# Last expert gathered an expert earlier, expert 30's part added in the last accumulation, biases in four parts, two more ring places

## The chip, the cores and the metric

The kernel runs on one core of a Trainium2 chip. The metric is the device time of one execution in microseconds (us). Three executions of the kernel before took 1175.88, 1176.34 and 1177.59 us. The profiled execution, from which all rows below come, took 1176.17 us, of which its trace covers a span of 1174.3 us from the first to the last instruction. All arithmetic is float32 unless a line says otherwise.

## The reference

256 tokens of 1024 numbers pass one layer: an attention-like mixer (an SSD group and an MLA group beside each other), then a mixture of experts. The second half is what the change touches.

```python
logits = h @ w_router + b_router
top_vals, top_idx = lax.top_k(logits, 4)          # 4 of 32 experts for each token
gates = softmax(top_vals)
...                                               # for each expert, its tokens xb and gates g:
gu = xb @ w_gate_up[e] + b_gate_up[e]             # 1024 -> 2 x 1024
glu = minimum(gu[:, :1024], 7.0); lin = clip(gu[:, 1024:], -7.0, 7.0)
act = glu * sigmoid(1.702 * glu) * (lin + 1.0)
y = act @ w_down[e] + b_down[e]                   # 1024 -> 1024
f += y * g                                        # added to the token's row
...
x = x + g2 * rms_norm(f, post_ffn_norm)
```

The weights of one expert are 8 MiB (w_gate_up) and 4 MiB (w_down). All 32 experts are read, so 384 MiB of the 427 MiB that the kernel reads are theirs.

## The kernel before, in words

**Front.** The mixer runs first, some 195 us. Its weights come as tiles of 1 MiB, and so do those of the experts. SP issues every load, in the order of one list, into one queue. A tile of the list has a place in SBUF. `Stream` (lines 72 to 105) holds the free places: a load is written into the program as soon as a place is free in program order. The mixer has 7 places (w0 to w6). While it ends, it hands on eleven buffers of its own (lines 1082, 1138, 1150), so the experts have 18. The order in which instructions stand on SP, DVE and ACT is then set by a scheduler that simulates the program; SP's loads go where the simulation has their place free. On PE the order is that of the program text from line 544 on.

**An expert, e.** Its tokens (up to 64; the rare rest is handled in a branch, `overflow`) are gathered by a matmul with a one-hot matrix, `gather(e)` (8 instructions at line 1173, each float32 matmul being two), transposed and scaled in `gathered(e)` (line 1181). `up` (line 1194) multiplies by the eight tiles gu0 to gu7 of w_gate_up; for each tile 4 matmuls, 8 instructions. `act` (lines 1207 to 1233) transposes the result on PE (line 1214, "tp"), and DVE and ACT make the activation `ac`. `down` (line 1242, "py") multiplies by the four tiles dn0 to dn6 of w_down. Rows of 64 slots are used: one matmul fills 64 of the 128 PSUM partitions.

**The loop.** Lines 1417 to 1469 run over the experts. In iteration e PE does: up on gu0 and gu1 of e, gather(e+1), down(e-1), up on gu2 and gu3, the transposes for e+1, up on gu4 to gu7, the branch, the transposes of act(e). After every even expert the results of the two experts before are added to the tokens: `scatter` (lines 1271 to 1278, "pc") makes four matmuls of 128 x 512, each followed by an addition to `acc` on DVE. The matrix for it, `gt`, comes from `spread_cols` (DVE) and `spread_mats` (four transposes, line 1266, and a copy on ACT). Expert 30 is different: down(29) is done at the start of its iteration, before up. In iteration 31 PE does down(30), copies it to `yl`, and scatters it alone (line 1437).

**The biases of w_down** (b_down) are added once for all experts: a matmul of the gates (32 experts as rows) with b_down, in the scatter of expert 24, ahead of each of its four matmuls (line 1276, 32 rows of the array). b_down and the gain of the last norm are loaded together as the tile `end`, ahead of expert 22's weights; it keeps its place in the ring to the end of the program.

**The end.** w_down of expert 31 comes in pieces by columns: 0 to 511, 512 to 767, 768 to 1023 (`parts`, line 1474). For each of the three and each half t of the tokens there is a PSUM bank `fin`. A matmul with the identity first puts `acc` into it (lines 1450 and 1498), and the last scatter (line 1483) adds expert 31. ACT sums the squares from `fin` (line 1484), DVE multiplies `fin` by the gain (line 1478), then come the norm, the addition to x and four stores.

Of the kernel before, what the change touches and what calls it, by code (L numbers as in the profile page):

```python
# [9 lines left out]
F32 = mybir.dt.float32  # L10
# [5 lines left out]
OP = mybir.AluOpType  # L16
# [5 lines left out]
P = 128  # L22
TT = S // P
# [83 lines left out]
def body(ctx, tc, a, out, ne=NE):  # L107
    nc = tc.nc
# [4 lines left out]
    def tl(shape, name, tag=None, dt=F32):  # L113
        tag = tag or name
        return sb.tile(shape, dt, tag=tag, name=name)
# [167 lines left out]
        return f  # L283

    for e in range(ne):
        if e == ne - 10:
            st_.want("end", ld_end)
        for k in range(KT):
            st_.want(f"gu{e}_{k}", ld(lambda t: t, w_gu[e][:, k, :]))
        for k in range(0, FT, 2):  # L290
            if e < ne - 1:
                st_.want(f"dn{e}_{k}", ld(halves, w_dn[e][:, k // 2]))
            else:
                st_.want(f"dn{e}_{k}", ld_last(k))
# [865 lines left out]

    mp = ctx.enter_context(tc.tile_pool(name="mp", bufs=1, space=PSUM))
    acc = tl([P, TT, D], "acc", "f1")
    iota = cst[:, CIO : CIO + CAP]

    def gather(e):
# [95 lines left out]
    def spread_mats(go):  # L1261
# [5 lines left out]
        gt = tl([P, 2, TT, P], "gtm", "bgr")  # L1267
        A.copy(gt, pg)
        return gt

    def scatter(lhs, rhs, bias=None, tag="pc", chs=(0, 1), ts=range(TT)):
        for t in ts:
            for ch in chs:
                pc = mp.tile([P, 512], F32, tag=tag, name="pc", bufs=2)
                if bias is not None:
                    T.matmul(pc, bias[:, t, :], end[0:NE, D + ch * 512 : D + ch * 512 + 512], start=True, stop=False)
                T.matmul(pc, lhs(t, ch), rhs(ch), start=bias is None, stop=True)  # L1277
                V.tensor_tensor(acc[:, t, ch * 512 : ch * 512 + 512], acc[:, t, ch * 512 : ch * 512 + 512], pc, op=OP.add)  # L1278

    def warm(n):  # L1280
# [136 lines left out]
    for e in range(ne):  # L1417
        wg = [st_.take(f"gu{e}_{k}") for k in range(KT)]
        wdp, wd = wd, weights_down(e)
        ahead = e in (0, 2, 3, last)  # L1420
        if e == last - 1:
            finish_down(e - 1, ac, wdp)
        if e == last:
            py = down(e - 1, ac, wdp, 0)
            yl = tl([P, 512], "yl", "pv2")
            A.copy(yl, py)
        gu = halves_of_up()
        tc.mark_branch_hint_location(f"more{e}", engines=[mybir.EngineType.PE])
        up(gu, xT, wg, range(0, 2))
        if ahead:  # L1430
            overflow(e, wg, wd, f"pr{(e + ahead) % 2}")
            for k in range(0, 2):
                st_.done(f"gu{e}_{k}")
        if e < last:
            xg = gather(e + 1)
        if e == last:
            scatter(lambda t, ch: gt[64 * ch : 64 * ch + 64, 0, t, :], lambda ch: yl[64 * ch : 64 * ch + 64, :])
        elif 0 < e < last - 1:
            finish_down(e - 1, ac, wdp)
        up(gu, xT, wg, range(2, 4))  # L1440
        if e < last:
            xTn = gathered(e + 1, xg)
        if e % 2 == 0:
            go = spread_cols((e, e, e + 1, e + 1) if e == last - 1 else (e, e + 1, e + 1, e))
        if e == ne - 7:
            g2b = gain()
        if e == last:
            fin = {(t, 1): mp.tile([P, 512], F32, tag="pc", name="fin", bufs=2) for t in range(TT)}
            for t in range(TT):
                T.matmul(fin[t, 1][:, 0:256], ident, acc[:, t, 512:768], start=True, stop=False)  # L1450
        up(gu, xT, wg, range(4, 8))
        xT = xTn
# [5 lines left out]
        if e == ne - 8:  # L1458
            end = st_.take("end")
            bias = gates_by_expert()  # L1460
        pair = e > 0 and e % 2 == 0
        if pair and e < last - 1:
            scatter(lambda t, ch: gt[:, ch, t, :], lambda ch: comb[ch], bias)
            bias = None
# [3 lines left out]
        if e % 2 == 0:  # L1468
            gt = spread_mats(go)


    tc.keep_in_program_order(A.activation(epsw, epsc, AF.Sqrt))
# [2 lines left out]

    def gained(t, i):
        c0, w = parts[i]
        V.tensor_tensor(acc[:, t, c0 : c0 + w], fin[t, i][:, 0:w], g2b[:, c0 : c0 + w], op=OP.mult)  # L1478

    def last_scatter(t, i, now=True):  # L1480
        c0, w = parts[i]
        fv = fin[t, i][:, 0:w]
        T.matmul(fv, gt[:, 1, t, :], yl[i], start=False, stop=True)  # L1483
        A.activation(scr[:, 0:w], fv, AF.Square, accum_out=ssf[:, t, i : i + 1])  # L1484
        if i == 0:
            V.tensor_scalar(ssf[:, t, 0:1], ssf[:, t, 0:1], 1.0 / D, EPS, op0=OP.mult, op1=OP.add)
        elif i == 1:
            V.scalar_tensor_tensor(ssf[:, t, 1:2], ssf[:, t, 1:2], 1.0 / D, ssf[:, t, 0:1], op0=OP.mult, op1=OP.add)  # L1488
        else:
            A.activation(ssf[:, t, 2:3], ssf[:, t, 2:3], AF.Sqrt, bias=ssf[:, t, 1:2], scale=1.0 / D)  # L1490
        if now:
            gained(t, i)

    for t in range(TT):
        for i, tag in ((0, "gu"), (2, "tp")):
            c0, w = parts[i]
            fin[t, i] = mp.tile([P, 512], F32, tag=tag, name="fin", bufs=2)
            T.matmul(fin[t, i][:, 0:w], ident, acc[:, t, c0 : c0 + w], start=True, stop=False)  # L1498
    ordered.__exit__(None, None, None)
    ordered = tc.manual_schedule(engines={mybir.EngineType.PE, mybir.EngineType.Activation, mybir.EngineType.DVE})  # L1500
    ordered.__enter__()
    yl = []
    for i, (c0, w) in enumerate(parts):
        py = mp.tile([P, 512], F32, tag=("py", "sm", "py")[i], name="pyl")
        for f0 in (0, 4):
            for f in range(f0, f0 + 4):
                g = f % 2
                wv = wd(f, c0 // 512)[:, c0 % 512 : c0 % 512 + w]
                T.matmul(py[64 * g : 64 * g + 64, 0:w], ac[:, f, :], wv, start=f < 2, stop=f >= 6)  # L1509
        yl.append(tl([P, w], f"yl{i}", ("pv2", "bn", "md1")[i]))  # L1510
        A.copy(yl[i], py[:, 0:w])
        if i:
            for t in range(TT):
                last_scatter(t, i - 1)
# [42 lines left out]
```

## Time and profile before

| | |
|---|---|
| median of three executions | 1176.34 us |
| the profiled execution | 1176.17 us, span 1174.3 us |
| PE busy (matmuls) | 1074.3 us, 91% of the span |
| DVE, ACT, POOL busy | 448.6, 190.8, 66.4 us |
| moved by DMA | 449.23 MB, 383 GB/s over the span |
| mean granted clock of TensorE | 0.961 of full speed |

PE (the matmul engine) and the DMA queue are both busy nearly throughout, so a share says little on which of them a stretch waits for. What is to be read is, for each stretch, whether the queue's rate falls (then it waits for a free place, and PE sets the pace), or whether PE stands still for a tile (then the queue sets it). [...]

### The profile page before, as it was taken

How to read it: one execution, taken by the hardware profiler on the slowest of the kernel's cores; microseconds unless marked ns; L12 is line 12 of the kernel's file. 1: busy time of each engine (PE TensorE's matmuls, PEld its weight loads, DVE VectorE, ACT ScalarE, POOL GpSimd, SP SyncE). 2: the span in 40 equal slices, each digit the busy share in tenths (PEclk: the TensorE clock that was granted, in tenths of full speed). 3: DMA queues.
4: the chain of work that ended last, by engine and by line, in shares of the span. 5: the costliest groups of instructions: out<-in, count | busy, mean ns of one | idle time of the engine just before them, and what ended most of it. 6: DMA issues, size and time to landing. Idle time of an engine off the chain costs nothing. (4 is left out here: it accounts for less than half of the span.)

```text
span 1174.3 us, 13394 instructions
## 1 busy us (share of the span) xinstructions
PE 1074.3 (91%) x5079; PEld 456.9 (39%) x5082; DVE 448.6 (38%) x921; ACT 190.8 (16%) x364; POOL 66.4 (6%) x68
## 2 busy tenths in 40 slices
PE   5899998989999999898989898989798999999897
PEld 4886774333333333232333232323233233333333
DVE  6968844333232323232323232323223133323233
ACT  5265442111110001010101010101001000111003
POOL 1254440000000000000000000000000000000000
PEclk9899999999999999898999898989899979999898
DMA  9968799779989999999999999999999998999992
GB/s 325 326 257 338 253 377 366 307 291 403 414 360 419 420 420 419 420 420 420 420 420 421 419 421 420 419 421 420 407 420 420 420 388 337 420 420 419 421 409 83
DMA packets 79915, 449.23 MB, mean 383 GB/s; under 512 B 10385, under 2 KB 23166, under 8 KB 29090
## 3 DMA queue, kind: packets, MB, share of 16 engines
q1 hardware_dynamic: 79362, 447.43, 94.0%
q8 instruction: 74, 1.21, 0.4%
q14 instruction: 63, 0.52, 0.1%
q10 hardware_dynamic: 416, 0.07, 0.0%
HBM read 446.42 MB, written 1.05 MB: 381 GB/s over the span
## 5 line engine op out<-in xcount | busy, mean ns | idle before, releaser
L1194 PE MATMUL gu<-gu,xT 128*64 128x512 f32 x2048 | 476.5, 613 | 36.7 <-DMA gu<-in_w_gate_up 35.2
L1194 PEld LDWEIGHTS gu<-gu,xT 128*64 128x64 f32 x2048 | 145.8, 141 | 317.8 <-issue 266.6
L1242 PE MATMUL py<-dn,ac 128*64 128x512 f32 x992 | 221.0, 598 | 5.7 <-DVE ac L1230 4.3
L1242 PEld LDWEIGHTS py<-dn,ac 128*64 128x64 f32 x992 | 71.9, 138 | 149.0 <-issue 135.1
L1251 DVE COPY cm<-py 64x512 f32<-64x512 f32 x30 | 20.8, 695 | 213.4 <-ACT cm L1250 213.4
L1200 DVE COPY gs<-gu 128x512 f32<-128x512 f32 x31 | 21.4, 691 | 168.1 <-PE gu L1194 168.1
L1277 PE MATMUL pc<-cm,gtm 128*128 128x512 f32 x120 | 63.0, 653 | 10.3 <-DVEq L1356 9.9
L1199 ACT COPY gs<-gu 128x512 f32<-128x512 f32 x32 | 18.8, 587 | 316.1 <-PE gu L1194 316.1
L1278 DVE TENSOR_TENSOR acc<-acc,pc 128x512 f32<-128x512 f32 x68 | 46.5, 687 | 59.0 <-PE pc L1277 58.9
L1173 PE MATMUL pg<-x,oh 128*64 128x512 f32 x256 | 60.5, 593 | 3.0 <-DVEq L1356 2.3
L1183 DVE TENSOR_TENSOR xT<-pgt,md 128x512 f32<-128x512 f32 x32 | 22.1, 692 | 90.6 <-PE pgt L1181 90.6
L1520 POOL TENSOR_TENSOR x<-x,acc 128x512 f32<-128x512 f32 x1 | 1.3, 1261 | 935.4 <-ACT acc L1519 935.4
L1169 DVE TENSOR_SCALAR oh<-cst,rkp,r 128x64 f32<-128x64 f32 x64 | 17.2, 312 | 84.8 <-PE pg L1173 84.8
L1221 DVE TENSOR_TENSOR u<-tp,biasT 128x512 f32<-128x512 f32 x64 | 41.6, 685 | 19.5 <-PE tp L1214 19.2
L1250 ACT COPY cm<-py 64x512 f32<-64x512 f32 x30 | 17.4, 581 | 194.1 <-PE py L1242 194.1
L1214 PEld LDWEIGHTS tp<-ident,gs 128*128 128x128 f32 x256 | 35.2, 207 | 29.8 <-ACTq L1356 17.6
L1214 PE MATMUL tp<-ident,gs 128*128 128x128 f32 x256 | 38.9, 293 | 6.9 <-PEq L1356 5.7
L1175 ACT COPY xg<-pg 128x512 f32<-128x512 f32 x32 | 18.8, 587 | 134.7 <-PE pg L1173 134.7
L1277 PEld LDWEIGHTS pc<-cm,gtm 128*128 128x128 f32 x120 | 19.9, 196 | 52.9 <-DVEq L1356 19.6
L1227 ACT ACTIVATE sg<-u 128x512 f32<-128x512 f32 (+1 forms) x33 | 20.4, 619 | 96.0 <-DVE u L1226 96.0
L1173 PEld LDWEIGHTS pg<-x,oh 128*64 128x64 f32 x256 | 18.2, 137 | 40.1 <-issue 39.4
L1258 DVE TENSOR_SCALAR go<-cst,rkp,gate 128x64 f32<-128x64 f32 x128 | 30.1, 309 | 0.6 <-DVEq L1356 0.6
(401 smaller groups left out, 962.7 us busy)
## 6 DMA issues: line engine op xcount, KB each, us to landing
gu<-in_w_gate_up SPq DMA_DIRECT2D x256, 1024.0 KB, 18.3
dn<-in_w_down SPq DMA_DIRECT2D x124, 1024.0 KB, 19.8
ada<-in_w_ada SPq DMA_DIRECT2D x16, 1024.0 KB, 5.2
mod<-in_w_ada SPq DMA_DIRECT2D x16, 512.0 KB, 9.4
xbc<-in_w_in SPq DMA_DIRECT2D x4, 1024.0 KB
wo<-in_w_out SPq DMA_DIRECT2D x4, 1024.0 KB
z<-in_w_in SPq DMA_DIRECT2D x2, 1024.0 KB, 6.8
dn<-in_w_down SPq DMA_DIRECT2D x4, 512.0 KB
```

The lines of the kernel that those rows point to most:

```text
L1173: T.matmul(pg[64 * h : 64 * h + 64, :], oh[:, t, :], x[:, t, h * 512 : h * 512 + 512], start=t == 0, stop=t == TT - 1)
L1183: V.tensor_tensor(xT.rearrange("p (h q) s -> p q h s", h=2), pg, a2.rearrange("p (h q) -> p q h", h=2)[:, :, :, None].to_broadcast([P, 4, ...
L1194: T.matmul(gu[h][64 * g : 64 * g + 64, :], xT[:, k, :], ws[k][:, g * 1024 + h * 512 : g * 1024 + h * 512 + 512], start=k == 0, stop=k == K ...
L1200: copy(gs[1], gu[1])
L1214: T.transpose(tp[f // 4][:, f % 4].rearrange("p g s -> p (g s)"), gs[f // 4][:, rows_of(f % 4)], ident)
L1221: V.tensor_tensor(u[:, hs], tp[h], bv[:, hs, :, None].to_broadcast([P, 4, 2, CAP]), op=OP.add)
L1227: A.activation(sg[:, fs], u[:, fs, 0, :], AF.Sigmoid, scale=1.702)
L1242: T.matmul(py[64 * g : 64 * g + 64, :], ac[:, f, :], wd(f, ch), start=f == 0, stop=f == FT - 1)
L1251: V.tensor_copy(comb[(e & 1) ^ 1][64:128, :], py[64:128, :])
L1258: V.tensor_scalar(go[:, t, j, :], iota, rkp[:, t, ee : ee + 1], gate[:, t, ee : ee + 1], op0=OP.is_equal, op1=OP.mult)
L1277: T.matmul(pc, lhs(t, ch), rhs(ch), start=bias is None, stop=True)
L1278: V.tensor_tensor(acc[:, t, ch * 512 : ch * 512 + 512], acc[:, t, ch * 512 : ch * 512 + 512], pc, op=OP.add)
```

## The change

1. Two tags, x0 and x1, are added to the ring's places (20 for the experts, not 18). The room for them comes from an option of the program, `dynamic_dma_scratch_size=256`.
2. The tile `end` is loaded ahead of expert 8. The bias is added in the scatters of experts 10, 12, 14 and 16, one of the four (t, ch) parts in each. The gates for it are transposed in iteration 9, the gain is made in iteration 19.
3. Expert 31 is gathered, and the scatter matrix of experts 30 and 31 made, at the end of iteration 29, between act(29) and down(29).
4. The scatter of expert 30 alone goes. Its product is put into `fin` instead, by matmuls of 64 rows, between act(31) and the last down. For the column parts 0 and 1 `acc` is no more put into `fin` by an identity matmul: DVE adds `fin` to `acc` in SBUF, and squares and gain are taken from there. Part 2 is as before, with one matmul more.

```diff
@@ body @@
-        if e == ne - 10:
+        if e == 8:
             st_.want("end", ld_end)
...
     acc = tl([P, TT, D], "acc", "f1")
+    st_.add("x0", "x1")
...
+    bias_left = [(t, ch) for t in range(TT) for ch in range(2)]
...
-                if bias is not None:
+                if bias is not None and (t, ch) == bias_left[0]:
                     T.matmul(pc, bias[:, t, :], end[0:NE, D + ch * 512 : D + ch * 512 + 512], start=True, stop=False)
-                T.matmul(pc, lhs(t, ch), rhs(ch), start=bias is None, stop=True)
+                T.matmul(pc, lhs(t, ch), rhs(ch), start=bias is None or (t, ch) != bias_left[0], stop=True)
...
-        if e < last:
+        if e < last - 1:
             xg = gather(e + 1)
-        if e == last:
-            scatter(lambda t, ch: gt[64 * ch : 64 * ch + 64, 0, t, :], lambda ch: yl[64 * ch : 64 * ch + 64, :])
-        elif 0 < e < last - 1:
+        if 0 < e < last - 1:
             finish_down(e - 1, ac, wdp)
...
-        if e == last:
-            fin = {(t, 1): mp.tile([P, 512], F32, tag="pc", name="fin", bufs=2) for t in range(TT)}
-            for t in range(TT):
-                T.matmul(fin[t, 1][:, 0:256], ident, acc[:, t, 512:768], start=True, stop=False)
...
+        if e == last - 2:
+
+            xTl = gathered(last, gather(last))
+            gtl = spread_mats(spread_cols((last - 1, last - 1, last, last)), "cbs")
...
     def gained(t, i):
         c0, w = parts[i]
-        V.tensor_tensor(acc[:, t, c0 : c0 + w], fin[t, i][:, 0:w], g2b[:, c0 : c0 + w], op=OP.mult)
+        src = fin[t, i][:, 0:w] if i == 2 else acc[:, t, c0 : c0 + w]
+        V.tensor_tensor(acc[:, t, c0 : c0 + w], src, g2b[:, c0 : c0 + w], op=OP.mult)
...
         T.matmul(fv, gt[:, 1, t, :], yl[i], start=False, stop=True)
+        if i < 2:
+            V.tensor_tensor(acc[:, t, c0 : c0 + w], acc[:, t, c0 : c0 + w], fv, op=OP.add)
+            fv = acc[:, t, c0 : c0 + w]
         A.activation(scr[:, 0:w], fv, AF.Square, accum_out=ssf[:, t, i : i + 1])
...
-    for t in range(TT):
-        for i, tag in ((0, "gu"), (2, "tp")):
-            c0, w = parts[i]
+    fin = {}
+    for i, tag in ((0, "gu"), (1, "pc"), (2, "tp")):
+        c0, w = parts[i]
+        ch = c0 // 512
+        for t in range(TT):
             fin[t, i] = mp.tile([P, 512], F32, tag=tag, name="fin", bufs=2)
-            T.matmul(fin[t, i][:, 0:w], ident, acc[:, t, c0 : c0 + w], start=True, stop=False)
+            fv = fin[t, i][:, 0:w]
+            if i == 2:
+                T.matmul(fv, ident, acc[:, t, c0 : c0 + w], start=True, stop=False)
+            T.matmul(fv, gt[64 * ch : 64 * ch + 64, 0, t, :], ylp[64 * ch : 64 * ch + 64, c0 % 512 : c0 % 512 + w], start=i < 2, stop=False)
...
-    nc = bacc.Bacc("TRN2", target_bir_lowering=False, num_devices=1)
+    nc = bacc.Bacc("TRN2", target_bir_lowering=False, num_devices=1, dynamic_dma_scratch_size=256)
```

Where the instructions stand, at three places. First SP's queue in the front, where before the second tile of w_in for the mixer (xbc_97) is followed by tiles of w_ada (mod) and w_in (nat):

```order
L212 DMA nat_93<-in_w_in 128x2x392
L213 DMA nat_93<-in_w_in 128x2x32
L214 DMA nat_93<-in_w_in 128x2x256
L181 DMA xbc_97<-in_w_in 128x2x1024
L191 DMA mod_192<-in_w_ada 128x4x256 x2
L191 DMA mod_199<-in_w_ada 128x4x256 x2
```

and now:

```order
L212 DMA nat_93<-in_w_in 128x2x392
L213 DMA nat_93<-in_w_in 128x2x32
L214 DMA nat_93<-in_w_in 128x2x256
L181 DMA xbc_97<-in_w_in 128x2x1024
L181 DMA gu_6_1773<-in_w_gate_up 128x2048
L181 DMA gu_7_1775<-in_w_gate_up 128x2048
L191 DMA mod_192<-in_w_ada 128x4x256 x2
L191 DMA mod_199<-in_w_ada 128x4x256 x2
```

The places x0 and x1 are free from the program's start, so the scheduler loads their first tiles, gu6 and gu7 of expert 1, early in the front, ahead of mod_192; before, these two loads stand behind the first expert's branch.

Second PE between the transposes of expert 29 (tp) and the weights of expert 30 (gu_0 to gu_4), with down(29) as py, before:

```order
L1214 MATMUL tp<-ident,gs_13245 128x128 x4
L1242 MATMUL py<-dn_0_13114,ac 64x512 x4
L1242 MATMUL py<-dn_2_13116,ac 64x512 x4
L1242 MATMUL py<-dn_4_13118,ac 64x512 x4
L1242 MATMUL py<-dn_6_13120,ac 64x512 x4
L1194 MATMUL gu<-gu_0_13122,xT 64x512 x4
L1194 MATMUL gu<-gu_1_13205,xT 64x512 x4
L1173 MATMUL pg<-x,oh 64x512 x4
L1194 MATMUL gu<-gu_2_13207,xT 64x512 x4
L1194 MATMUL gu<-gu_3_13209,xT 64x512 x4
L1181 MATMUL pgt<-ident,xg 128x128 x4
L1194 MATMUL gu<-gu_4_13211,xT 64x512 x4
```

and now:

```order
L1215 MATMUL tp<-ident,gs_13249 128x128 x4
L1174 MATMUL pg<-x,oh 64x512 x4
L1182 MATMUL pgt<-ident,xg 128x128 x4
L1267 MATMUL pgt<-ident,go 128x128 x4
L1243 MATMUL py<-dn_0_13114,ac 64x512 x4
L1243 MATMUL py<-dn_2_13116,ac 64x512 x4
L1243 MATMUL py<-dn_4_13118,ac 64x512 x4
L1243 MATMUL py<-dn_6_13120,ac 64x512 x4
L1195 MATMUL gu<-gu_0_13122,xT 64x512 x4
L1195 MATMUL gu<-gu_1_13124,xT 64x512 x4
L1195 MATMUL gu<-gu_2_13126,xT 64x512 x4
L1195 MATMUL gu<-gu_3_13209,xT 64x512 x4
```

The gather (pg), its transposes (pgt of xg) and the four transposes for the scatter matrix (pgt of go, before in iteration 30) now stand ahead of down(29).

Third PE from the transposes of expert 31 to the last down (pyl), before:

```order
L1214 MATMUL tp<-ident,gs_14359 128x128 x4
L1498 MATMUL fin<-acc,ident 128x512
L1498 MATMUL fin<-acc,ident 128x256
L1498 MATMUL fin<-acc,ident 128x512
L1498 MATMUL fin<-acc,ident 128x256
L1509 MATMUL pyl<-dn_0_13903,ac 64x512 x4
```

and now:

```order
L1215 MATMUL tp<-ident,gs_14343 128x128 x4
L1514 MATMUL fin<-yl,gtm 128x512 x2
L1514 MATMUL fin<-yl,gtm 128x256 x2
L1513 MATMUL fin<-acc,ident 128x256
L1514 MATMUL fin<-yl,gtm 128x256
L1513 MATMUL fin<-acc,ident 128x256
L1514 MATMUL fin<-yl,gtm 128x256
L1525 MATMUL pyl<-dn_0_13910,ac 64x512 x4
```

Two identity matmuls of 512 columns have gone, and six matmuls of expert 30's result (yl) have come; the first two read partitions 0 to 63, the other four 64 to 127.

## Rows read from the trace of the kernel before

**Rows 1.** Windows. Busy us of engines, granted clock, DMA share, GB/s:

```profile
225.00:345.00 120.00, 113.36 (x570) 43.00 (x572) 40.22 (x81) 11.47 (x20) 0.42 (x1) 1.00 0.86 349
345.00:930.00 585.00, 537.49 (x2401) 189.98 (x2398) 180.46 (x351) 52.41 (x88) 0.00 (x0) 0.96 1.01 420
954.00:981.00 27.00, 26.60 (x128) 9.47 (x126) 10.24 (x23) 2.60 (x5) 0.00 (x0) 1.00 0.74 294
```

**Rows 2.** Timeline, PE: experts 10, 24, 28 begin. Start, us, [idle before <-releaser]:

```profile
480.54 6.07 PE L1194 MATMUL gu<-gu,xT 128*64 128x512 f32 x16 [3.22 <-DMA gu<-in_w_gate_up]
...
908.73 5.31 PE L1194 MATMUL gu<-gu,xT 128*64 128x512 f32 x16 [3.39 <-DMA gu<-in_w_gate_up]
...
1033.59 3.65 PE L1194 MATMUL gu<-gu,xT 128*64 128x512 f32 x16
```

**Rows 3.** Timeline, PE: scatters of experts 10 and 24:

```profile
507.28 3.89 PE L1277 MATMUL pc<-cm,gtm 128*128 128x512 f32 x8 [1.06 <-DVEq L1356]
...
935.63 1.75 PE L1276 MATMUL pc<-end,gT 32*128 32x512 f32 x2 [0.45 <-ACT gT L1379]
...
951.19 1.91 PE L1214 MATMUL tp<-ident,gs 128*128 128x128 f32 x8
```

**Rows 4.** Windows: the scatter of expert 24:

```profile
936.00:951.00 15.00, 15.00 (x16) 3.73 (x15) 2.07 (x3) 0.00 (x0) 0.00 (x0) 0.50 1.02 422
```

**Rows 5.** Windows: the start of the program:

```profile
0.00:28.60 28.60, 14.75 (x76) 13.26 (x76) 19.50 (x43) 16.56 (x23) 3.33 (x5) 1.00 0.98 325
18.00:48.00 30.00, 25.83 (x157) 24.89 (x157) 28.03 (x40) 9.74 (x12) 6.30 (x2) 0.89 1.08 369
```

**Rows 6.** Timeline, SP and DVE: mod_192 issued, and first used:

```profile
18.17 5.94 SPq L191 DMA_DIRECT2D mod<-in_w_ada  x4
...
34.05 0.48 DVE L451 TENSOR_SCALAR md<-mod,cact 128x512 f32<-128x512 f32 x1
```

**Rows 7.** Timeline, PE: from expert 29's transposes to the last down:

```profile
1086.67 1.20 PE L1214 MATMUL tp<-ident,gs 128*128 128x128 f32 x8 [0.40 <-PEq L1356]
1091.96 9.28 PE L1242 MATMUL py<-dn,ac 128*64 128x512 f32 x32 [4.10 <-DVE ac L1230]
...
1104.50 1.90 PE L1173 MATMUL pg<-x,oh 128*64 128x512 f32 x8
...
1117.84 1.19 PE L1214 MATMUL tp<-ident,gs 128*128 128x128 f32 x8 [0.40 <-PEq L1356]
...
1124.81 7.09 PE L1242 MATMUL py<-dn,ac 128*64 128x512 f32 x32 [1.37 <-DVEq L1356]
...
1135.63 1.13 PE L1277 MATMUL pc<-yl,gtm 64*128 64x512 f32 x4 [0.30 <-PEq L1356]
...
1139.15 3.65 PE L1194 MATMUL gu<-gu,xT 128*64 128x512 f32 x16
1142.74 1.13 PE L1450 MATMUL fin<-acc,ident 128*128 128x256 f32 x4
...
1152.15 2.75 PE L1498 MATMUL fin<-acc,ident 128*128 128x512 f32 x8
1154.83 5.38 PE L1509 MATMUL pyl<-dn,ac 128*64 128x512 f32 x32
```

**Rows 8.** Windows: the wait ahead of down(29), and its first half:

```profile
1090.00:1096.00 6.00, 4.04 (x10) 1.39 (x12) 1.39 (x2) 0.26 (x1) 0.00 (x0) 0.50 1.02 421
```

**Rows 9.** Timeline, ACT and DVE: squares, gain, and the first reciprocal:

```profile
1161.30 0.60 ACT L1484 ACTIVATE scr<-fin 128x512 bf16<-128x512 f32 x1 [0.67 <-PE fin L1483]
...
1162.09 0.68 DVE L1478 TENSOR_TENSOR acc<-fin,end 128x512 f32<-128x512 f32 x1
...
1165.31 0.42 DVE L1478 TENSOR_TENSOR acc<-fin,end 128x256 f32<-128x256 f32 x1
...
1166.59 0.15 DVE L1525 RECIPROCAL ssf<-ssf 128x1 f32<-128x1 f32 x1
```

**Rows 10.** DMA queues: kind, packets, MB, share of 16 engines:

```profile
q1 hardware_dynamic: 79362, 447.43, 94.0%
```

More of the change, by code (lines that the diff above doesn't have):

```diff
@@ L1259, in spread_cols, with spread_mats @@
         return go
-    def spread_mats(go):
+    def spread_mats(go, tag="bgr"):
         pg = mp.tile([P, 2, TT, P], F32, tag="sm", name="pgt")
@@ L1424, in body @@
             py = down(e - 1, ac, wdp, 0)
-            yl = tl([P, 512], "yl", "pv2")
-            A.copy(yl, py)
+            ylp = tl([P, 512], "yl", "pv2")
+            A.copy(ylp, py)
         gu = halves_of_up()
@@ L1433, in body @@
                 st_.done(f"gu{e}_{k}")
-        if e < last:
+        if e < last - 1:
             xg = gather(e + 1)
-        if e == last:
-            scatter(lambda t, ch: gt[64 * ch : 64 * ch + 64, 0, t, :], lambda ch: yl[64 * ch : 64 * ch + 64, :])
-        elif 0 < e < last - 1:
+        if 0 < e < last - 1:
             finish_down(e - 1, ac, wdp)
         up(gu, xT, wg, range(2, 4))
-        if e < last:
+        if e < last - 1:
             xTn = gathered(e + 1, xg)
-        if e % 2 == 0:
-            go = spread_cols((e, e, e + 1, e + 1) if e == last - 1 else (e, e + 1, e + 1, e))
-        if e == ne - 7:
+        if e % 2 == 0 and e < last - 1:
+            go = spread_cols((e, e + 1, e + 1, e))
+        if e == 19:
             g2b = gain()
-        if e == last:
-            fin = {(t, 1): mp.tile([P, 512], F32, tag="pc", name="fin", bufs=2) for t in range(TT)}
-            for t in range(TT):
-                T.matmul(fin[t, 1][:, 0:256], ident, acc[:, t, 512:768], start=True, stop=False)
         up(gu, xT, wg, range(4, 8))
-        xT = xTn
+        xT = xTn if e < last - 1 else xTl
         gs = up_out(gu, "g1b", A.copy if e == last else V.tensor_copy)
@@ L1457, in body @@
             st_.done(f"gu{e}_{k}")
-        if e == ne - 8:
+        if e == 9:
             end = st_.take("end")
@@ L1463, in body @@
             scatter(lambda t, ch: gt[:, ch, t, :], lambda ch: comb[ch], bias)
-            bias = None
+            if bias is not None:
+                bias_left.pop(0)
+                bias = bias if bias_left else None
         ac = act(e, gs, 2 if e == last else 1)
@@ L1467, in body @@
             scatter(lambda t, ch: gt[:, ch, t, :], lambda ch: comb[ch])
-        if e % 2 == 0:
+        if e == last - 1:
+            gt = gtl
+        elif e % 2 == 0:
             gt = spread_mats(go)
+        if e == last - 2:
+            xTl = gathered(last, gather(last))
+            gtl = spread_mats(spread_cols((last - 1, last - 1, last, last)), "cbs")
     tc.keep_in_program_order(A.activation(epsw, epsc, AF.Sqrt))
@@ L1509, in body @@
                 T.matmul(py[64 * g : 64 * g + 64, 0:w], ac[:, f, :], wv, start=f < 2, stop=f >= 6)
-        yl.append(tl([P, w], f"yl{i}", ("pv2", "bn", "md1")[i]))
+        yl.append(tl([P, w], f"yl{i}", ("bn", "pt0", "md1")[i]))
         A.copy(yl[i], py[:, 0:w])
```

2 lines of the change are left out of this document (1 added, 1 removed).

## The prediction

> **What bounds the kernel now.** I read windows of the whole expert phase first, to find where the queue is slower than it can be. It moves 420 GB/s from 345 to 930 us [rows 1], so a tile of 1 MiB takes 1.049 MB / 420 GB/s = 2.50 us and an expert of twelve takes 30.0. From 225 to 345 us it moves only 349 GB/s: 120 x 71/420 = 20.3 us of the queue are lost there. From 954 to 981 it moves 294: 27 x 126/420 = 8.1 us lost. In such a stretch SP waits for a free place, and PE, busy all the time, sets the pace. In between PE waits for the queue: at the beginning of expert 10 it stood 3.22 us for gu0, at 24 for 3.39, and at 28 there is no such idle time [rows 2]. The even experts are the ones that wait, so I read the loop in pairs: (908.73 - 480.54) / 7 = 61.17 us each. Of this span the load of `end` (160 rows of 1024 numbers, 0.66 MB, 1.6 us) is taken once, which leaves 60.9. That is more than two times 30.0, as the tile that comes last at its slowest DMA engine slides back a little in each expert.
>
> The timeline of PE shows what happens at 936. The usual scatter takes 3.89 us; in expert 24 the eight bias matmuls of 32 rows alternate with the eight others, and from the first to the next transposes there are 951.19 - 935.63 = 15.56 us [rows 3]. [...] PE so loses 15.56 - 3.89 = 11.7 us, the ring fills, and the queue stands 8.1 us. From here PE is behind the queue, and sets the time to the end.
>
> **Two places.** In the early stretch, where PE is the bound, each further place lets the queue run one tile ahead: 2 x 2.50 = 5.0 us, all of it inside the 20.3 that are lost there. Against it stands the new place of the first two of these loads, ahead of mod_192: everything behind them in SP's queue is 5.0 us later. The queue moved 325 GB/s up to 28.6 us [rows 5], 9.3 MB, which is where mod_192's last byte stands by its place in the list. mod_192 is issued from 18.17 on and first used by DVE at 34.05 [rows 6]. That leaves 34.05 - 28.6 = 5.4 us, a little more than the 5.0. In this stretch DVE is busy 28.03 of 30 us, PE 25.83 and the queue is full (1.08) [rows 5], so it is near both limits. I charge 0.5 us for it (bounds: 0, if the slack holds, and 5.0, if all that follows is late in full). Sum: experts are loaded 4.5 us earlier from expert 9 on (bounds 0 and 5.0).
>
> **The biases.** One bias matmul (two instructions) in each of four scatters at full clock costs under 1 us, and falls in experts 10 to 16, where PE waits for the queue anyway: nothing. If it dropped the clock each time, the price would be a part of the 11.7 us, some 3 us, and each such expert's wait of 3.22 covers it. In expert 24 the 11.7 us go, and with them the 8.1 us of stall. What is late next is the queue itself: expert 28 can start at 908.73 - 4.5 + 2 x 60.9 = 1026.0 instead of 1033.59, 7.5 us earlier (with 59.9 for a pair: 9.6 earlier; with the front 5 us late: 3.1). As it then begins with a wait, its first two tiles take 5.31 to 6.07 us as in experts 24 and 10, not 3.65 [rows 2]: +2.1 on average. Expert 29's transposes are 5.4 us earlier.
>
> **Expert 29's end.** PE waits 4.10 us for `ac` behind these transposes, and down(29) takes 9.28 us instead of the 7.09 of down(30) [rows 7], as the clock stands at 0.50 from 1090 to 1096 [rows 8]. The gather (1.90), its transposes and those of the scatter matrix (half of 1.19 for each four) are 3.1 us and fit into that wait: they cost nothing there, the clock stays up (-2.2), and gather and transposes no more stand in expert 30 (-2.5). Their copies on ACT and DVE come between the operations of `ac`; I charge 0.5. Sum -4.2 (bounds -2.0, if the clock falls all the same, and -4.7). Nothing else on PE waits behind them: the next tile has long been there.
>
> **Expert 30.** PE waited 1.37 us for `ac` after the scatter of 28 and 29 and the transposes for the scatter matrix [rows 7]. DVE has an addition less ahead of it: about one addition of 512 columns, 0.68 [rows 9], less what the queue in front of DVE keeps; -0.55 (bounds 0, -1.4).
>
> **Expert 31.** The scatter of 30 alone goes: 1139.15 - 1135.63 = 3.5 us with its wait for DVE. So does the first identity matmul, 1.1 [rows 7]. Sum -4.6; nothing hid them, since PE is the bound.
>
> **Ahead of the last down** the identity matmuls took 2.75 us for 2 x 512 and 2 x 256 columns [rows 7], 0.23 us for 256 columns of one instruction pass. Now there are 20 such passes instead of 12: 4.6 us one after another. The scatter of `yl` shows that passes on the two halves of the array overlap: four of 512 took 1.13 [rows 7], where four of full height take half of 3.89 [rows 3]. Here only the end of the first group (rows 0 to 63) borders on the second (64 to 127), so at most four passes of 20 are hidden: 3.7. I take +1.3, between +0.9 and +1.8.
>
> [...]
>
> **The tail.** For parts 0 and 1 DVE now adds first, ACT squares the sum, DVE takes the square's result and makes the gain, one after another by the order of DVE's queue. From 1161.30 for each half of part 0: 0.68 + 0.79 + 0.15 + 0.68 = 2.3; of part 1, with 0.42 for 256 columns and 0.6 for the square: 1.6; and one more gain of 0.42 [rows 9]. 2 x 2.3 + 2 x 1.6 + 0.4 = 8.2, less 0.3 for small overlaps, gives the first reciprocal at 1169.2 in place of 1166.59: +2.6 (bounds +0.7, one addition alone, and +2.9).
>
> **Sum** against the profiled execution: -5.4 - 4.2 - 0.55 - 4.6 + 1.3 + 2.6 = -10.85, so a span of 1163.4 and a time of 1176.17 - 10.85 = 1165.3 us. The median of the runs shown, 1176.34, is the same within 0.02%.
>
> **The rivals.** *The slide stops.* If the arrivals keep the mean rate, 59.9 us for a pair, expert 28 starts 9.6 us earlier, and with little or no wait: 1161 to 1163. For it: the slide was 1 us a pair in one execution, and the order of loads is another one. Against: it was there in all seven pairs.
>
> *The front is late in full.* The 5.4 us of slack are worked out from a mean rate, and the loads are striped over 16 engines whose last one counts. Then the two places bring nothing, 4.5 us are lost of the sum: 1169.8. Against: DVE at 28.03 of 30 [rows 5] has work that doesn't need mod_192.
>
> *The last down at half clock.* The eight bias matmuls of 32 rows ran at 0.50, and the wait of 4.10 us was followed by it too [rows 4, 8]. If the matmuls of 64 rows, or a wait for `ac` beside them, bring it on, the first pyl (5.38 us) and the tp wait take up to twice as long: +4 to +7, so 1169 to 1172. Against: the `yl` scatter of 64 rows is followed by gu at 3.65, full speed [rows 7].
>
> *Slower: the weight stream suffers from the smaller scratch.* [...] If the queue of the weights used it, its rate would fall in the whole expert phase: 402.7 MB at 420 GB/s are 959 us, so each per cent is 9.6 us, and from 1.1% on (a rate under 415) all of the gain is eaten; at 2% the time is 1184. For it: this queue carries nearly everything. Against: the table lists it as hardware_dynamic with 447.43 MB [rows 10], whereas the few others, 1.8 MB, are of another kind. [...]
>
> *The biases do nothing.* If the stall at 954 stays, from another cause, expert 28 starts only the 4.5 us of the ring earlier, without the 2.1 of low clock: -4.5 in place of -5.4, 1166.2. So this part's size hardly shows in the total.
>
> **How the numbers follow.** Forecast (with the last rival, which ends beside it) 55%, its own terms reaching from about 1162 to 1168.5. The slide stops 15%, the front late in full 12%, half clock at the end 8%, slower stream 6%, anything else 4%. The first four end faster by over 0.2% (2.4 us, about what a measurement of this kernel can tell from no change), which makes 0.90; of these I move 0.02 to no change, for two mishaps at once, and split the rest: faster 0.88, same 0.05, slower 0.07. The range 1159 to 1172 takes in the cases up to half clock.
>
> **What would show it.** Right: windows of 225 to 345 at a higher rate than 349 GB/s; a scatter of 24 near 3.9 us and no stretch at 0.50 there; no stall after 954; expert 28 beginning with a wait near 1026; from tp(29) to tp(30) some 27 us instead of 31.2, with down(29) near 7.1; fins of 3.7 to 4.6 us ahead of pyl; the first reciprocal 14.4 us behind pyl's start, where it was 11.8 [rows 7, 9]. Wrong: the mixer's md later than 34.05 by some us and all after it; the queue under 415 GB/s between 345 and 930; a clock under 1.00 at pyl; expert 28 starting at once, which means that PE and not the queue sets the pace there.

## The result, and the profile after

The changed kernel takes 1165.03 us (median of four runs, 1163.41 to 1165.69), the kernel before 1176.96 beside it (four runs, 1175.88 to 1179.47): a ratio of 0.9894, 95% interval 0.9878 to 0.9911. On another chip the same kernel came to 0.9904 (0.9883 to 0.9926). The profiled execution took 1165.31 us with a span of 1163.5, 10.86 less than the one before; 10.85 was forecast. The sum is right to the tenth, its terms are not: two of them missed by 2 us each, in opposite directions. Two of the kernels below each had one execution far outside the others (2941.03 us for the new end alone, 3809.75 us for the biases whole); it is in neither their medians nor their ratios.

First the windows of the kernel after, with the columns of [rows 1]:

```profile
225.00:345.00 120.00, 113.57 (x573) 43.12 (x573) 39.70 (x79) 11.30 (x20) 0.42 (x1) 1.00 0.85 348
345.00:930.00 585.00, 544.03 (x2435) 192.40 (x2432) 182.83 (x357) 53.36 (x91) 0.00 (x0) 0.97 1.01 420
930.00:954.00 24.00, 24.00 (x110) 8.99 (x112) 10.76 (x23) 2.38 (x4) 0.00 (x0) 1.00 1.01 423
954.00:981.00 27.00, 22.23 (x96) 7.56 (x94) 5.72 (x10) 2.38 (x4) 0.00 (x0) 0.87 1.01 418
```

The stretch at half clock (0.50 in [rows 4]; from 930 to 954 it is 1.00 now) and the stall behind it are gone, 418 GB/s for the 294 of [rows 1]. The 0.87 of the last row belongs to the first tiles of expert 26, behind a wait. The early stretch still runs at 348 GB/s: two more places don't raise a rate that PE sets, they put the queue two tiles further ahead. (The prediction asked for a higher rate there; that sign was chosen wrongly.)

PE at the starts and scatter that answer to [rows 2, 3], and expert 26:

```profile
903.03 6.18 PE L1195 MATMUL gu<-gu,xT 128*64 128x512 f32 x16 [3.89 <-DMA gu<-in_w_gate_up]
...
929.86 3.89 PE L1281 MATMUL pc<-cm,gtm 128*128 128x512 f32 x8 [1.03 <-DVEq L1360]
...
964.39 5.79 PE L1195 MATMUL gu<-gu,xT 128*64 128x512 f32 x14 [4.37 <-DMA gu<-in_w_gate_up]
...
1023.86 1.68 PE L1195 MATMUL gu<-gu,xT 128*64 128x512 f32 x4 [2.57 <-DMA gu<-in_w_gate_up]
```

Expert 24 begins 5.7 us earlier (4.5 forecast), and expert 28 waits for its tile as forecast, at 1023.86 instead of 1026.0. From there, what answers to [rows 7]:

```profile
1078.96 1.21 PE L1215 MATMUL tp<-ident,gs 128*128 128x128 f32 x8 [0.40 <-PEq L1360]
1080.09 1.94 PE L1174 MATMUL pg<-x,oh 128*64 128x512 f32 x8
1083.07 0.66 PE L1182 MATMUL pgt<-ident,xg 128*128 128x128 f32 x4 [1.04 <-ACT xg L1176]
1084.65 0.66 PE L1267 MATMUL pgt<-ident,go 128*128 128x128 f32 x4 [0.92 <-DVE xT L1184]
1085.24 8.78 PE L1243 MATMUL py<-dn,ac 128*64 128x512 f32 x32
...
1108.16 1.20 PE L1215 MATMUL tp<-ident,gs 128*128 128x128 f32 x8 [0.40 <-PEq L1360]
...
1135.50 1.49 PE L1215 MATMUL tp<-ident,gs 128*128 128x128 f32 x8
1136.92 1.98 PE L1514 MATMUL fin<-yl,gtm 64*128 64x512 f32 x8
1138.83 0.70 PE L1513 MATMUL fin<-acc,ident 128*128 128x256 f32 x2
1139.46 0.70 PE L1514 MATMUL fin<-yl,gtm 64*128 64x256 f32 x2
1140.09 0.70 PE L1513 MATMUL fin<-acc,ident 128*128 128x256 f32 x2
1140.71 0.70 PE L1514 MATMUL fin<-yl,gtm 64*128 64x256 f32 x2
1141.34 5.38 PE L1525 MATMUL pyl<-dn,ac 128*64 128x512 f32 x32
```

The wait of 4.10 us ahead of down(29) is filled, but not without gaps: PE waits 1.04 us for the copy of `xg`, then 0.92 for DVE's `xT`, and down(29) still takes 8.78. A window of 1085 to 1090 gives a clock of 0.66, 1090 to 1095 again 1.00. And the tail, DVE behind the last down, against [rows 9]:

```profile
1147.82 0.69 DVE L1492 TENSOR_TENSOR acc<-acc,fin 128x512 f32<-128x512 f32 x1 [7.47 <-PE fin L1490]
1149.35 0.15 DVE L1496 TENSOR_SCALAR ssf<-ssf 128x1 f32<-128x1 f32 x1 [0.85 <-ACT scr L1494]
1149.42 0.68 DVE L1485 TENSOR_TENSOR acc<-acc,end 128x512 f32<-128x512 f32 x1
1150.02 0.68 DVE L1492 TENSOR_TENSOR acc<-acc,fin 128x512 f32<-128x512 f32 x1
1151.55 0.15 DVE L1496 TENSOR_SCALAR ssf<-ssf 128x1 f32<-128x1 f32 x1 [0.85 <-ACT scr L1494]
...
1155.58 0.15 DVE L1541 RECIPROCAL ssf<-ssf 128x1 f32<-128x1 f32 x1
```

The first reciprocal comes 14.24 us behind the start of pyl (14.4 forecast, 11.76 before): DVE adds, waits 0.85 us for ACT's square, makes the gain, and only then adds the other half.

One table serves all experiments. It is worked out from each trace: the start of expert 0's first up (the front's length), then, counted from there, the starts of experts 24 and 28 and of the transposes (tp) of expert 29; then the pieces to tp(30), tp(31), the first pyl and the end of the span. All in us; the kernels below "after" are those of the experiments.

```
kernel            front   e24    e28    tp29   29-30 30-31 31-pyl pyl-end
before            189.71  719.03 843.88 896.97 31.17 32.98  4.01  19.45
before again      187.92  719.00 843.56 896.64 30.96 32.98  4.01  19.45
after             190.22  712.81 833.64 888.74 29.20 27.34  5.84  22.19
after again       188.32  712.62 833.48 888.65 27.50 28.55  5.85  22.19
places            191.16  712.99 834.78 889.80 31.47 35.03  4.01  19.44
biases            189.94  720.45 842.50 897.87 31.64 32.98  4.01  19.45
places + biases   189.00  714.06 835.87 891.11 31.58 35.03  4.01  19.45
new end           187.35  719.01 841.02 896.02 29.20 28.07  5.84  21.92
late places       192.65  712.56 834.38 889.56 27.50 27.58  5.85  22.19
biases whole      191.12  714.54 836.32 891.33 27.50 27.84  5.85  21.93
tail              190.86  714.67 836.46 891.50 27.51 27.74  5.85  20.24
fins              192.58  713.99 835.10 889.91 29.15 27.35  5.45  22.19
mats first        192.88  713.20 834.10 889.16 26.29 29.86  5.85  22.18
all three         190.79  714.51 836.37 891.92 26.29 28.37  5.45  20.24
```

The front varies by 5 us between these executions (187.35 to 192.88) with no order in it, and this is why the columns start behind it. Where one kernel has two traces, it makes most of their difference in time: 1.8 of 2.3 us for the kernel before, 1.9 of 2.5 for the one after.

### The profile page after: what moved, and what is told of

The parts are those of the page before. It is cut to its first block, busy times and chain, and to the rows that moved or that the text cites. A ratio compares the mean times of both kernels' runs of the same rounds, so it can differ in the third digit from the quotient of the medians.

```text
span 1163.5 us, 13379 instructions
## 1 busy us (share of the span) xinstructions
PE 1064.9 (92%) x5078; PEld 452.4 (39%) x5078; DVE 446.1 (38%) x921; ACT 190.5 (16%) x364; POOL 68.1 (6%) x68
## 5 line engine op out<-in xcount | busy, mean ns | idle before, releaser
L1282 DVE TENSOR_TENSOR acc<-acc,pc 128x512 f32<-128x512 f32 x64 | 44.0, 687 | 39.7 <-PE pc L1281 39.6
```

## The experiments

Theory A: the queue of weights has a lead over PE, made early by the places, and sets the starts of the even experts to 28; what PE loses in expert 24 it mostly gets back by waiting less. Theory B: the time gained is PE's lost time of expert 24 given back.

**Places alone** (e1_places).

```diff
     acc = tl([P, TT, D], "acc", "f1")
+    st_.add("x0", "x1")
...
-    nc = bacc.Bacc("TRN2", target_bir_lowering=False, num_devices=1)
+    nc = bacc.Bacc("TRN2", target_bir_lowering=False, num_devices=1, dynamic_dma_scratch_size=256)
```

> The kernel before with the two places x0 and x1 alone (and the smaller scratch that makes room for them). Theory A (loads run 4.5 us ahead once, and this lead lasts as long as the queue is full): expert 24 begins some 4 to 5 us before 908.7, its bias scatter still takes 15.6 us and the queue still stands some 8 us behind it; from there PE sets the pace, so the end is 4.5 us earlier: about 1172. Theory B (the gain of the changed kernel is the 11.7 us of PE in expert 24 given back; the places bring nothing): no change, 1176 to 1177. If the smaller scratch slowed the stream, it would show as less than 420 GB/s from 345 to 930 us and a time above 1177.

1173.6 us (12 runs) beside 1177.65; ratio 0.9970 (0.9952 to 0.9989), -3.5 us. Expert 24 begins 6.0 us earlier than before in the table. The queue's bytes give the lead directly: at the beginning of expert 0 it has landed 5.7 us x 420 GB/s more than in the kernel before, 100 us later 5.0 (the two tiles), and by 700 us 6.1. The stream is not slower: 420 GB/s from 345 to 900. Theory B falls, and with it the rival of the scratch memory. What was not expected stands in the scatter of expert 24, the same instructions as before:

```profile
930.78 1.12 PE L1277 MATMUL pc<-end,gT 32*128 32x512 f32 x2 [0.45 <-ACT gT L1380]
931.84 1.12 PE L1278 MATMUL pc<-cm,gtm 128*128 128x512 f32 x2
...
938.15 1.12 PE L1278 MATMUL pc<-cm,gtm 128*128 128x512 f32 x2
939.12 1.11 PE L1215 MATMUL tp<-ident,gs 128*128 128x128 f32 x8
```

8.3 us, not 15.6, at full clock (1.00 from 930 to 954), behind the same idle 0.45 us.

**Biases alone** (e2_biases): `end` ahead of expert 8, one of the four parts in each of experts 10 to 16.

```diff
-        if e == ne - 10:
+        if e == 8:
             st_.want("end", ld_end)
...
-                if bias is not None:
+                if bias is not None and (t, ch) == bias_left[0]:
```

> The kernel before with the biases alone in four parts in experts 10 to 16 (end loaded ahead of expert 8). Theory A: the 11.7 us of PE and the stall of the queue at 954 go, but then expert 28 has to wait for its tile, at 908.7 + 2 x 60.6 to 60.9 = 1030 to 1030.5 in place of 1033.6, and its first two tiles run at half clock (+2): 1 to 1.7 us faster only, about 1175. Theory B: the 11.7 us come back in full, about 1165.

1177.53 us (12 runs); ratio 1.0000 (0.9982 to 1.0019). Expert 28 begins with a wait, tp(29) is no earlier than before: the 11.7 us aren't in the time. Some 1.8 us of this trace are another event: the first two tiles of expert 0 took 5.35 us instead of 3.65, about as long as the 5.31 at the start of expert 24 in [rows 2] with a granted clock of 0.50 in its first 3.4 us. They came behind the same idle 1.51 us as before, and as PE is the bound there, the queue stood 1.8 us behind that of the kernel before once 60 us had passed.

**Both** (e3_places_biases): the two diffs above in one kernel.

> The kernel before with the places and the biases, and the old end. Theory A: expert 28 begins near 1024 with a wait, expert 29's transposes are 7.7 us earlier as in the changed kernel, and the end with them: about 1169, more than the two parts alone add up to (4.5 + 1 to 1.7). Theory B: 11.7 us faster, about 1165, as the biases alone.

1172.01 us (10 runs); ratio 0.9951 (0.9934 to 0.9968), -5.8 us. More than the places alone (0.9970), but the intervals overlap, and short of the 8 us that theory A expected. It has the same event at the start (1.8 us of lead). The 35.03 from tp(30) to tp(31), here and with the places alone, are 2 us over the 32.98 before: the scatter of 28 and 29 waits for DVE's additions (1.04 and 0.80 us), and 3.4 us at half clock follow (0.83 over the 10 us from 1115 with both), up to the first half of down(30); no trace of a kernel with the new end has that stretch.

**The new end alone** (e4_end): expert 31 gathered in iteration 29 and expert 30 added in the last accumulation, on 18 places and the old biases, with the scratch memory of before.

```diff
-    st_.add("x0", "x1")
...
-        if e == 8:
+        if e == ne - 10:
...
-                if bias is not None and (t, ch) == bias_left[0]:
+                if bias is not None:
```

(against the changed kernel)

> The kernel before with the new end alone (expert 31 gathered in iteration 29, expert 30's part in the last accumulation), 18 places and the old biases. If the terms at the end are local, as read from the changed kernel's trace against the one before (-2.0 to expert 30's transposes, -5.6 to expert 31's, +1.8 to the last down, +2.5 and +0.2 behind it): 3.1 us faster, about 1173.3. If they depend on what the places and biases do (PE further behind the queue or not), something else: with the clock up in down(29) up to 5.5 us faster, 1171.

1174.44 us (11 runs); ratio 0.9971 (0.9956 to 0.9986), -3.4 us, as the terms read from the trace give (-3.1). The pieces of the table repeat those of the changed kernel (29.20, 28.07, 5.84, 21.92). Up to expert 28 this kernel has the instructions of before, and its scatter of expert 24 ran at full clock (1.00 from 930 to 954), with 391 GB/s behind it in place of 294. Expert 28 then begins at 841.0 with a wait, not 843.9 without; tp(29) differs by 0.9 us only.

**Before once more** (e5_before_again), unchanged.

> The kernel before once more, unchanged, for a second trace of it. In the first one the bias scatter of expert 24 ran at half clock (15.6 us and a stall of the queue); in the two kernels so far that kept these instructions it took 8.3 us at full clock. If the half clock belongs to the instructions and the place, it is here again: 15.6 us, 294 GB/s behind it, expert 28 near 1033 without a wait. If it was an event of that one execution: 8.3 to 8.4 us, 420 GB/s behind it, and expert 28 begins with a wait near 1030 (908.7 + 2 x 60.6 to 60.9).

1173.85 us (one run). The half clock is there again, from the second pair of matmuls on:

```profile
935.16 1.12 PE L1276 MATMUL pc<-end,gT 32*128 32x512 f32 x2 [0.45 <-ACT gT L1379]
936.21 1.45 PE L1277 MATMUL pc<-cm,gtm 128*128 128x512 f32 x2
937.59 2.07 PE L1276 MATMUL pc<-end,gT 32*128 32x512 f32 x2
...
947.60 2.08 PE L1277 MATMUL pc<-cm,gtm 128*128 128x512 f32 x2
949.47 1.57 PE L1214 MATMUL tp<-ident,gs 128*128 128x128 f32 x8
```

and its windows, with the stall:

```profile
930.00:954.00 24.00, 22.41 (x58) 7.49 (x56) 6.80 (x15) 2.02 (x4) 0.00 (x0) 0.72 1.01 416
954.00:981.00 27.00, 26.60 (x128) 9.45 (x126) 10.06 (x19) 2.52 (x5) 0.00 (x0) 1.00 0.76 300
```

So of five traces with this scatter (the fifth is that of the biases whole, below), two (both of the kernel before) fell to half clock and three (with other kernels' places or end) did not, with the same idle time ahead. Neither reading of the expectation holds alone: the event recurs, but the instructions and the idle time ahead of them don't bring it on by themselves. What decides it stays open.

**After once more** (e6_after_again), unchanged, beside the next two.

> The changed kernel once more, unchanged, so that the next kernels have it beside them on one chip. If its parts add up as measured alone (places and biases -0.49%, new end -0.29%): ratio 0.992 to the kernel before. If 0.9894 holds on this chip too, 0.989.

1165.77 us (6 runs) beside 1177.20; ratio 0.9904 (0.9883 to 0.9926). Both expectations lie in the interval. Its profiled execution, 1162.84 us, is 11.0 below that of the kernel before once more on this chip. In its trace down(29) takes 7.09, not 8.78, behind the same two gaps, and tp(29) to tp(30) is 27.5: the 2.2 us of the prediction come in this execution, not in the first. But most of them don't reach the end:

```profile
1121.36 7.09 PE L1195 MATMUL gu<-gu,xT 128*64 128x512 f32 x32 [0.16 <-PEq L1360]
1128.66 1.94 PE L1195 MATMUL gu<-gu,xT 128*64 128x512 f32 x8 [0.21 <-DMA gu<-in_w_gate_up]
1131.15 1.94 PE L1195 MATMUL gu<-gu,xT 128*64 128x512 f32 x8 [0.55 <-DMA gu<-in_w_gate_up]
1133.02 1.50 PE L1215 MATMUL tp<-ident,gs 128*128 128x128 f32 x8
```

PE now waits for the last tiles of expert 31.

**Late places** (e7_late_places).

```diff
+    for tg in ("x0", "x1"):
+        V.tensor_copy(sb.tile([P, 2048], F32, tag=tg, name="hold")[:, 0:NE], rkp[:, 1, :])
     st_.add("x0", "x1")
```

> The changed kernel, with x0 and x1 held until the router's ranks are known (an operation of DVE writes into each of them), so that gu6 and gu7 of expert 1 are no more loaded ahead of mod_192 but after the front. Theory A (the early loads cost the front 0.5 us, and the lead of the queue comes from the number of places, not from loading these two early): 0.5 us faster than the changed kernel on the same chip, expert 0 beginning 0.5 us earlier. Rival (the lead is the two tiles that are in already when the experts begin, since the queue can't load more than it does from 190 to 225): 4 to 5 us slower than the changed kernel.

1165.81 us (6 runs), ratio 0.9900 (0.9876 to 0.9924): the same as the changed kernel. The rival falls: at the beginning of expert 0 the queue is only 0.8 us ahead of the kernel before, 36 us later 5.5, and expert 24 begins at 712.56 as in the changed kernel. The lead comes from the number of places. The 0.5 us of the front can't be told from a front that varies by 5: that term stays open. What the early loads do to mod_192 can be seen: its first use on DVE, at 34.05 us in the first trace of before and 32.86 in the second, came at 36.06 and 35.38 in the two of the changed kernel and comes at 34.39 here.

**Biases whole** (e8_biases_whole): the changed kernel with the biases of before, in expert 24.

```diff
-        if e == 8:
+        if e == ne - 10:
             st_.want("end", ld_end)
...
-                if bias is not None and (t, ch) == bias_left[0]:
+                if bias is not None:
```

> The changed kernel with the biases of before: in expert 24 alone, four matmuls, end loaded ahead of expert 22. If the half clock at 936 in the first trace of before was an event of one execution: PE needs 8.3 instead of 3.9 us in this scatter, which the wait ahead of expert 26 or 28 takes in, and the time is the changed kernel's within 1 us. If the bias scatter falls to half clock as a rule: 15.6 us, a stall of the queue of 5 us or more, and the time 3 to 6 us above the changed kernel's.

1167.72 us (5 runs), ratio 0.9921 (0.9894 to 0.9947) beside 0.9904: unclear. In the trace the scatter ran at full clock (1.00 from 930 to 954), and tp(29) is at 891.33, 2.6 behind the changed kernel, of which 1.8 are the slow start of expert 0 (5.35 us for 3.65) that the biases alone showed too. At most 1 us is left for the biases.

The last four, beside one another on one chip, ask what the three terms that had been mis-sized consist of, and whether it can be had back. The changed kernel itself was not run on that chip: the ratios are to the kernel before, and the pieces of the traces are set against the changed kernel's traces from elsewhere.

**Tail** (e9_tail). `stat` is what followed the square in `last_scatter`.

```diff
             for t in range(TT):
                 last_scatter(t, i - 1)
+            for t in range(TT):
+                stat(t, i - 1)
```

> The changed kernel, with DVE's order behind the last down altered: both halves' additions of a part first, then both halves' scaling of the sum and gains (before: addition, scaling, gain for one half, then for the other, so that DVE waits for ACT's square of the first half before it adds the second). If the 2.5 to 2.7 us that the tail has become longer are this chain: from the start of pyl to the end 22.2 falls by about 1.8, to 20.4. If they are the additions' own time (2.2 us): no change.

1165.24 us (6 runs), ratio 0.9882 (0.9862 to 0.9902). From pyl to the end 20.24 for 22.19, -1.95. DVE behind the last down:

```profile
1149.93 0.69 DVE L1492 TENSOR_TENSOR acc<-acc,fin 128x512 f32<-128x512 f32 x1 [7.48 <-PE fin L1490]
1150.79 0.69 DVE L1492 TENSOR_TENSOR acc<-acc,fin 128x512 f32<-128x512 f32 x1 [0.17 <-PE fin L1490]
1151.47 0.15 DVE L1500 TENSOR_SCALAR ssf<-ssf 128x1 f32<-128x1 f32 x1
...
1155.74 0.15 DVE L1547 RECIPROCAL ssf<-ssf 128x1 f32<-128x1 f32 x1
```

The second addition stands ahead of the first scaling, and the two waits of 0.85 for ACT are gone. The four additions themselves cost no more than 0.8 us against before (20.24 to 19.45).

**Fins** (e10_fins).

```diff
             if i == 2:
-                T.matmul(fv, ident, acc[:, t, c0 : c0 + w], start=True, stop=False)
+                T.matmul(fin[t, i][:, 0:w], ident, acc[:, t, c0 : c0 + w], start=True, stop=False)
+        for t in range(TT):
+            fv = fin[t, i][:, 0:w]
```

> The changed kernel, with the eight instructions of the third column part in the order identity, identity, yl, yl instead of identity, yl, identity, yl: two changes between 128 and 64 rows fewer. From expert 31's transposes to pyl it is 5.85 us; the four groups of two take 0.63 each, where their passes alone, at 0.23, take 0.46. If a change between heights costs the 0.17 each: 0.3 to 0.4 us less. If it is the height or the start of a group in itself: no change.

1165.73 us (6 runs), ratio 0.9894 (0.9876 to 0.9913). From tp(31) to pyl 5.45 for 5.85:

```profile
1140.41 1.98 PE L1515 MATMUL fin<-yl,gtm 64*128 64x512 f32 x8
1142.32 1.13 PE L1512 MATMUL fin<-acc,ident 128*128 128x256 f32 x4
1143.38 1.13 PE L1515 MATMUL fin<-yl,gtm 64*128 64x256 f32 x4
1144.44 5.38 PE L1526 MATMUL pyl<-dn,ac 128*64 128x512 f32 x32
```

Four passes in one group take 1.06, in two groups 1.26: 0.2 us for each of the two changes of height taken away. The PSUM bank changes inside a group as well, so it is not the bank that costs this.

**Mats first** (e11_mats_first).

```diff
-            xTl = gathered(last, gather(last))
-            gtl = spread_mats(spread_cols((last - 1, last - 1, last, last)), "cbs")
+            gtl = spread_mats(spread_cols((last - 1, last - 1, last, last)), "cbs", "pc", 2)
+            xTl = gathered(last, gather(last))
```

(the last two arguments name the PSUM bank of these transposes and how many there are of it)

> The changed kernel, with the transposes for the scatter matrix of 30 and 31 ahead of the gather of 31, in a bank of their own, so that they no more wait for the bank that DVE frees after the activation. In the changed kernel down(29) starts 6.28 us after the transposes of 29, though its activation is there after some 5.0. If that wait is the cause of what was missing: 5.0 to 5.2, and from the transposes of 29 to those of 30 26.2 to 26.4 us instead of 27.5 (29.2 where the clock was down). If the activation itself is late: no change.

1165.52 us (6 runs), ratio 0.9894 (0.9877 to 0.9912). Down(29) starts 5.07 us behind its transposes, and tp(30) follows in 26.29:

```profile
1082.05 1.21 PE L1215 MATMUL tp<-ident,gs 128*128 128x128 f32 x8 [0.40 <-PEq L1360]
1083.09 0.60 PE L1267 MATMUL pgt<-ident,go 128*128 128x128 f32 x4
1083.62 1.94 PE L1174 MATMUL pg<-x,oh 128*64 128x512 f32 x8
1086.24 0.66 PE L1182 MATMUL pgt<-ident,xg 128*128 128x128 f32 x4 [0.69 <-ACT xg L1176]
1087.12 1.08 PE L1243 MATMUL py<-dn,ac 128*64 128x512 f32 x4 [0.22 <-DVE ac L1231]
```

But from tp(30) to tp(31) it is 29.86 instead of 27.34 to 28.55: three waits of 0.56 for the tiles of expert 31. From the front to tp(31) all is 945.31, against 945.28 and 944.70 in the two traces of the changed kernel. The queue sets this point; PE's 1.2 us are waited away.

**All three** (e12_all_three).

> The changed kernel with the three alterations together: about 3.4 us faster than the changed kernel (1.8 in the tail, 0.4 ahead of pyl, 1.2 at down(29)) if they add up, as all three lie where PE or the tail alone sets the end. If the last tiles come too late for a faster PE: expert 31's last gu tiles wait, and less than 2 us.

1164.20 us (5 runs) beside 1178.49, ratio 0.9874 (0.9855 to 0.9893), on that chip 1.0 us below the tail alone and 1.3 to 1.5 below the other two. From tp(31) to the end 25.69 for 28.03 in the changed kernel, -2.34, the 1.95 and the 0.40 added; of the 1.2 nothing. It is the fastest of the kernels run, but its interval overlaps that of the changed kernel: in the trace the gain is plain, in the time not.

## Why the prediction was right, and where it was not

**The time** was right: -10.85 forecast, -10.86 between the profiled executions, -11.0 between the second pair of them, -11.9 between the medians. That it fits to 0.01 us is luck: two misses of 2 us cancel, and the executions differ among themselves by more. Counted step by step from [rows 2, 7]:

| step | forecast | between the two traces |
|---|---|---|
| places and biases, to tp(29) | -5.4 | -7.7 |
| tp(29) to tp(30) | -4.2 | -2.0 |
| tp(30) to tp(31) | -5.15 | -5.6 |
| tp(31) to pyl | +1.3 | +1.8 |
| pyl to the end | +2.6 | +2.7 |

**Places** (step "two places", -4.5): right in mechanism, too small. In the four traces in which PE lost no further time early (places, after, after again, late places) the lead is 5.0 to 5.3 us 100 us into the experts, as worked out, late or early loads alike, and 6.0 to 6.5 by expert 24; in the other kernels with the two places it is 4.4 to 5.8 there. What the 1.1 more are due to wasn't tried. The rest of what this step and the next missed lies between experts 24 and 28, where the two pairs took 120.83 us and not 2 x 60.9 = 121.8. Of the late front there is a sign, mod_192 used at 36.06 and 35.38 us for 34.05 and 32.86, but expert 0 began only 0.5 and 0.4 us later, pair by pair.

**Biases** (step "the biases", 11.7 us and a stall, -0.9 in the sum): read from one execution. The half clock of [rows 4] recurs in the kernel before but isn't bound to these instructions. That its loss turns into the queue's wait at expert 28 was the right part: with half clock tp(29) is at 896.6 to 897.0, without it, in the new end alone, at 896.0. The rival "the biases do nothing" is near the truth in size (ratio 1.0000 alone), but not in its condition: the stall went.

Why a stall of 8 us is worth so little can be read from the traces, though no experiment asked for it. Each tile of 1 MiB lands in 16 parts. In both traces of the kernel before, the last part of a tile lands some 2 us behind its first near 345 us and 12 us behind it near 890, and behind the stall it is 2 us again. In the changed kernel, which has no stall, it goes on to 14 us near 1010. Experts 20, 24 and 28 of the changed kernel begin 0.04 to 0.05 us behind the last part of their first tile, so it is the part that slides back, the "slide" of the prediction, that they wait for. Over the stall of the kernel before, from 969 to 992 us, the last parts lost only 2.5 us against their rate of 2.5 us a tile: most of the 8.1 us was time that the other parts spent waiting.

**Expert 29's end** (step -4.2): the term that failed. "They cost nothing there, the clock stays up" held in the second trace of the changed kernel and not in the first. The bounds (-2.0 if the clock falls all the same) held. In the seven traces with the changed kernel's order here, behind the same two gaps, the clock fell in three (8.6 to 8.8 us for down(29)) and not in four (7.1). What I had not seen is that PE still waits 1.96 us in two pieces, 1.04 for ACT's copy of the gather and 0.92 because the second set of transposes needs the bank of the first; and that a faster PE is of little use by expert 31, because the queue's last tiles come no earlier: of the 1.8 us by which tp(30) came earlier in the second trace, 0.6 are left at tp(31). The four kernels that begin expert 24 late, at 714.0 to 714.7 (biases whole, tail, fins, all three), show the same: tp(31) comes 946.4 to 946.8 us behind the front whether tp(29) to tp(30) took 26.29 us or 29.15. "PE sets the time to the end" fails there, by about 1 us.

**Experts 30 and 31** (steps -0.55 and -4.6): right. Down(30) starts 0.76 us earlier behind tp(30), and from there to tp(31) it is 4.88 us less.

**Ahead of pyl and in the tail**: +1.8 is the upper bound named, but not for the reason that the bound had, no overlap. The first twelve passes took 1.91 us, not the 2.8 of twelve times 0.23, so the four that could overlap did, which alone would give +0.9. Most of the other 0.9 are the changes of height, which the sum had left out: the four groups behind took 0.63 us each, where their passes alone take 0.46. With two changes fewer (fins), 0.4 us went, 0.2 a change. The tail (+2.6, measured +2.7) was worked out as a chain through DVE and ACT, and breaking the chain took 1.95 of its 2.7.

**The slower rival** is excluded: 420 GB/s with the smaller scratch, as without. (Of the 1.8 MB that the prediction calls of another kind, 0.07 are of the same kind; nothing hangs on it.)

## What to carry to other kernels

Ask of each stretch who sets its end, and count a saving only there: places in the ring pay where PE is the bound (5 us here, kept for 700), while 6 to 7 us of PE's clock lost where the queue is the bound cost less than one here. A stretch at half clock in one profile needs a second profile before it is priced, and a dip in a queue's mean rate is a loss only as far as the last parts of its tiles land later for it (2.5 us of 8.1 here). In a tail, order the work of an engine so that nothing it can do already stands behind what waits for another engine (1.95 us on DVE here).

## What the runs showed of the hardware

The granted clock fell behind the same idle time in one execution and not in the next. The bias scatter behind 0.45 us of idle time took 15.6 and 14.3 us in the two traces of the kernel before (0.50 from 936 to 951 in the first, 0.72 from 930 to 954 in the second) and 8.3 in the three where the clock stayed at 1.00; down(29) behind the same two gaps took 8.6 to 8.8 us in three traces and 7.1 in four. In [rows 4] it stayed at 0.50 through the alternating 32-row and 128-row matmuls, with PE busy for 15.00 of 15.00 us. What brings it on, no run here shows.

A change between matmuls of 64 and of 128 rows cost 0.2 us (four passes took 1.26 us in two groups, 1.06 in one). With `dynamic_dma_scratch_size=256` the loads issued by SP moved 420 GB/s from 345 to 930 us, as without it. In a queue kept full for 550 us, the last of a tile's 16 parts fell back from 2 to 12 us behind the first, and a stretch at 294 GB/s brought it to 2 again; why, no run here shows.
